# Decayed queries and keys of the retention staged for their stores in three tiles of their own

## The chip, the cores and the metric

The kernel runs on one core of a Trainium2 chip. The metric is the device time of one execution in microseconds (us): 1528.29 us before the change, the median of three runs (1525.65 to 1530.34 us).

## The reference, cut to what matters

One encoder layer over 1024 tokens of width 1024, all in float32: a mixer (dilated window attention in 8 heads beside a two-directional retention in 4 heads), a cross attention to 256 memory tokens, and a mixture of 32 experts. The change touches the first stage of the mixer, which makes the operands of the retention:

```
proj = h @ w_in                        # columns: aq, ak, av, rq, rk, rv, rg
qr = split_heads(rq)                   # 4 heads of 64
kr = split_heads(rk) * 64 ** -0.5
k_dec = exp(lg * (C - 1 - i))          # the key's decay to its chunk's end
chunk_kv = einsum(kr, k_dec, vr)
q_dec = exp(lg * (i + 1))              # the query's decay from its chunk's start
y_cross = einsum(qr, q_dec, prev)
...
```

Both decays exist forward and backward (`lg` per head and direction). The kernel makes `qr * q_dec` and `kr * k_dec` once, in the projection stage, and keeps them in DRAM until the retention heads load them.

## The kernel before, in words

Every matmul of float32 data is done in three passes over values split into a high part (rounded to the matmul's format by a copy on ScalarE, ACT) and a low part (value minus high part, a subtraction on VectorE, DVE, or on GpSimd, POOL): high times high, low times high, high times low. The helper `split` (lines 110 to 113) writes both parts; `mm3` (119 to 122) issues the three matmuls. So ACT's L112 and the subtraction's L113 stand for all splits, told apart by their tiles, and TensorE's (PE's) L120 to L122 stand for all such matmuls.

The first stage (lines 318 to 660) makes 48 units in a loop, 8 for each of the six 512-column blocks of `w_in`: queries (`unit_qk`, c = 0), keys (c = 1), values (`unit_v`, c = 2), retention queries and keys (`unit_rqk`, c = 3), retention values (`unit_rv`, c = 4) and gates (`unit_rg`, c = 5). A unit is 24 matmuls on PE into one bank of PSUM (tag "mm", five banks, used in turn), a "chain" that empties the bank, and for some a "tail" with PE transposes, traced one unit later. The weights of the next block are split by `W.split` (L116 on ACT, L117 on DVE) into the four slots that the present block's last unit sets free, pair by pair.

A unit of `unit_rqk` with j = 0 to 3 is a query unit, with j = 4 to 7 a key unit. Query unit: the bank is split into a tile `spr`, stored to `rT_s` by two DMAs; then, for each direction, DVE multiplies the bank by the decay table into `qd` (L451, a "po" tile of three), `qd` is split into a tile `spqd` (ACT, POOL) and stored to `qd_s` by four DMAs. After the second `qd` the bank is empty. Key unit: `spr` likewise, a plain copy `kf` (L447, ACT, a "po" tile too) which empties the bank, and in the tail four PE transposes of `kf` (`tkd`, L465), eight multiplications into two tiles `kd` (L471), each split into a tile `kt` (ACT, POOL) and stored to `kd_s` by one DMA (L475).

All of `spr`, `spqd`, `kt`, the value units' `vt` (six DMAs each) and the retention values' `rvt` (four each) are tiles of one tag, "sp", in the pool `st`: two buffers of 4 KB per partition, given out in turn. A tile can be written when all the DMAs that read the tile two before it have landed. All stores and loads are issued by SyncE's queue (SP) in one order.

The pool `sl` ("p1late", line 632) holds what belongs to this part of the stage, `kd` and the decay tables among it; it is closed at s_ = 33, and the next pool there ("head0", line 651) takes its place in SBUF, with the first attention head's keys, values and queries.

This stage has no order written out by hand (only its first units have). A planner at build time puts each engine's instructions in order: of what its own model takes to be ready, what stands first in the program. On the chip each engine then runs its queue strictly in that order. So the order in which PE meets the matmuls of a unit and the transposes `tkd` is the planner's.

Of the kernel before, what the change touches and what calls it, by code (L numbers as in the profile page):

```python
# [11 lines left out]
F32R = mybir.dt.float32r  # L12
# [8 lines left out]
P = 128  # L21
# [18 lines left out]
GN_EPS = 1e-5  # L40
NEG = -1e30
PADJ = 16
KW = S + 2 * PADJ


@with_exitstack
def kernel(
# [270 lines left out]
    with ExitStack() as c1:  # L318
# [47 lines left out]
        def store2(dst, src_h, src_l):  # L366
            nc.sync.dma_start(dst[0], src_h.bitcast(F32))
            nc.sync.dma_start(dst[1], src_l.bitcast(F32))

        def parts(tag, name):  # L370
            t = st.tile([P, 4, 2, P], F32R, tag=tag, name=name).rearrange("p a i c -> p (a i c)")
            return [t[:, 512 * i:512 * i + 512] for i in range(2)]

        xts = {}
# [37 lines left out]
        def side_by_side(name):  # L412

            return st.tile([P, 4, 2, P], F32R, tag="sp", name=name)
# [20 lines left out]
        def unit_rqk(c, j):  # L435
            f, half = divmod(j, 2)
            isk, rp = divmod(f, 2)
            hs = slice(512 * half, 512 * half + 512)
            ps = bank("mm", 5, f"prqk{f}{half}")
            kf = st.tile([P, 512], F32, tag="po", bufs=3, name=f"kf{f}{half}") if isk else None  # L440

            def chain():
                h, l = parts("sp", f"spr{f}{half}_")
                split(h, l, ps)
                store2([t[f * P:f * P + P, hs] for t in rT_s], h, l)
                if isk:
                    act.activation(kf, ps, AF.Copy)  # L447
                    return
                for d in range(2):
                    qd = st.tile([P, 512], F32, tag="po", bufs=3, name=f"qd{f}{half}{d}")  # L450
                    dve.tensor_tensor(qd.rearrange("p (c i) -> p c i", c=2), ps.rearrange("p (c i) -> p c i", c=2),  # L451
                                      Gq[rp][:, d][:, None, :].to_broadcast([P, 2, 256]), OP.mult)
                    h, l = parts("sp", f"spqd{f}{half}{d}_")
                    split(h, l, qd, pool)
                    for j in range(2):
                        hh = 2 * rp + j
                        rows = slice(64 * j, 64 * j + 64)
                        store2([t[P * hh + 64 * d:P * hh + 64 * d + 64, hs] for t in qd_s], h[rows], l[rows])

            def tail():  # L460
                if not isk:
                    return
                pt = bank("tr", 3, f"tkd{f}{half}")
                for i in range(4):
                    pe.transpose(pt[:, i * P:i * P + P], kf[:, i * P:i * P + P], ident)  # L465
                ptv = pt.rearrange("p (c a h d) -> p a c h d", c=2, a=2, h=2)
                for j in range(2):
                    kd = sl.tile([P, 4, 2, 64], F32, tag="kd", name=f"kd{f}{half}{j}")
                    for a in range(2):
                        for d in range(2):  # L470
                            dve.tensor_scalar(kd[:, a::2, d], ptv[:, a, :, j], Gk[rp][:, a, d, j:j + 1], None,  # L471
                                              op0=OP.mult)
                    kt = side_by_side(f"kt{f}{half}{j}")
                    split(kt[:, :, 0], kt[:, :, 1], kd.rearrange("p t d e -> p t (d e)"), pool)
                    nc.sync.dma_start(kd_s[2 * rp + j, :, 4 * half:4 * half + 4],  # L475
                                      kt.rearrange("p t i c -> p t (i c)").bitcast(F32))
            return lambda: projT(ps, W.w[c], f, half), chain, tail
# [1897 lines left out]
```

## Time and profile before

| what | value |
| --- | --- |
| median of three runs | 1528.29 us (1525.65 to 1530.34) |
| the profiled execution | 1529.57 us, span 1527.6 us |
| PE busy | 1470.6 us, 96% of the span |
| VectorE, ScalarE, GpSimd busy | 75%, 58%, 15% |
| granted PE clock, mean | 0.988 |
| first stage (projections) | 0 to about 300 us |
| retention queries and keys on PE (c = 3) | 159 to 204 us |
| experts | about 950 us to the end |

Times in all rows are microseconds from the start of the span. The profiled execution's own time is its span and 2.0 us around it.

### The profile page before, as it was taken

The numbers are of one execution on the slowest core, as the hardware profiler recorded it, in microseconds if no ns is written. First come the engines' busy times: TensorE is split into PE (matmuls) and PEld (weight loads), VectorE is DVE, ScalarE is ACT, GpSimd is POOL, SyncE is SP. The second block draws the span as 40 slices with busy tenths as digits, with TensorE's granted clock in tenths as the row PEclk, the third lists the DMA queues.
The fourth block names the chain that finished last, engine by engine and source line by source line (L and its number), as shares of the span: only waits on it lengthen the run. The fifth ranks groups of instructions, "written<-read, shape, count | busy, mean of one in ns | idle before, by whom it ended". The sixth has DMA issues, their size and how long they took to land. (4 is left out here: it accounts for less than half of the span.)

```text
span 1527.6 us, 22387 instructions
## 1 busy us (share of the span) xinstructions
PE 1470.6 (96%) x7722; PEld 1171.7 (77%) x7722; DVE 1144.2 (75%) x2557; ACT 887.7 (58%) x1493; POOL 234.7 (15%) x204
## 2 busy tenths in 40 slices
PE   8999999999989999999999998999999999999995
PEld 7788878798978877888878886777777777776663
DVE  8865355287766675978675678899898899888894
ACT  6431233298862243733352325888888888877783
POOL 0000134234310000000000002222222222221111
PEclk9999999999999999999999998999999999999998
DMA  8446775779578884621235728999999999999992
GB/s 303 112 124 193 207 232 161 207 215 253 174 216 276 321 293 134 239 100 42 60 137 201 287 96 300 337 353 362 368 377 364 357 364 370 364 358 358 364 381 84
DMA packets 129109, 383.64 MB, mean 251 GB/s; under 512 B 16288, under 2 KB 49312, under 8 KB 110560
## 3 DMA queue, kind: packets, MB, share of 16 engines
q1 hardware_dynamic: 120624, 360.27, 67.9%
q0 software_dynamic: 8368, 21.91, 5.7%
q8 instruction: 62, 1.02, 0.3%
q14 instruction: 55, 0.45, 0.1%
HBM read 318.81 MB, written 71.70 MB: 256 GB/s over the span
## 5 line engine op out<-in xcount | busy, mean ns | idle before, releaser
L120 PE MATMUL p<-eh,x 128*96 128x512 f32 x384 | 154.0, 401 | 0.0
L122 PE MATMUL p<-el,x 128*96 128x512 f32 x384 | 152.3, 396 | 0.0
L121 PE MATMUL p<-eh,x 128*96 128x512 f32 x384 | 151.8, 395 | 0.0
L1684 POOL DMA_INDIRECT xg<-h_s,idx x32 | 77.4, 2420 | 277.3 <-PE xt L1694 276.5
L113 DVE TENSOR_TENSOR el<-ews,eh 128x1024 fp32r<-128x1024 f32 x86 | 100.9, 1219 | 15.7 <-ACT eh L112 15.7
L112 ACT ACTIVATE eh<-ews 128x1024 fp32r<-128x1024 f32 x86 | 87.4, 1054 | 21.8 <-DMA ews<-in_w_down_dram 10.6
L113 DVE TENSOR_TENSOR el<-ex,eh 128x1024 fp32r<-128x1024 f32 x74 | 86.8, 1217 | 3.9 <-PE xt L1694 1.8
L122 PEld LDWEIGHTS p<-el,x 128*96 128x96 f32 x384 | 62.5, 163 | 27.1 <-issue 0.5
L121 PEld LDWEIGHTS p<-eh,x 128*96 128x96 f32 x384 | 62.7, 163 | 25.7 <-DVE x L113 0.4
L120 PEld LDWEIGHTS p<-eh,x 128*96 128x96 f32 x384 | 62.4, 162 | 24.8 <-ACT x L112 0.2
L112 ACT ACTIVATE eh<-ex 128x1024 fp32r<-128x1024 f32 x74 | 75.5, 1054 | 9.6 <-PE p L121 4.7
L1767 POOL DMA_INDIRECT out_dram<-yo,idx x32 | 51.3, 1604 | 174.0 <-ACT yo L1766 169.4
L113 DVE TENSOR_TENSOR el<-wraws,eh 128x1024 fp32r<-128x1024 f32 x60 | 70.2, 1218 | 3.0 <-ACT eh L112 2.1
L112 ACT ACTIVATE eh<-wraws 128x1024 fp32r<-128x1024 f32 x60 | 60.4, 1054 | 5.5 <-DMA wraws<-in_w_up_dram 2.6
L113 DVE TENSOR_TENSOR ehl<-ex,ehl 128x1024 fp32r<-128x1024 f32 x50 | 58.7, 1215 | 0.0
L1766 ACT ACTIVATE yo<-py,lists 96x512 f32<-96x512 f32 x64 | 42.9, 684 | 25.8 <-PE py L122 25.5
L112 ACT ACTIVATE ehl<-ex 128x1024 fp32r<-128x1024 f32 x50 | 51.9, 1058 | 6.2 <-PE py L122 5.5
L120 PE MATMUL po<-woh,mx 128*128 128x512 f32 x128 | 51.8, 405 | 3.5 <-ACT mx L112 1.8
L113 DVE TENSOR_TENSOR ehl<-ews,ehl 128x1024 fp32r<-128x1024 f32 x44 | 51.9, 1218 | 2.4 <-ACT ehl L112 2.4
L120 PE MATMUL y<-VW,pT 128*128 128x512 f32 x128 | 53.0, 414 | 0.0
L112 ACT ACTIVATE ehl<-ews 128x1024 fp32r<-128x1024 f32 x44 | 45.8, 1057 | 11.5 <-PE py L122 5.5
L120 PE MATMUL py<-ehl,hm 128*96 128x512 f32 x128 | 52.2, 408 | 0.0
(844 smaller groups left out, 4464.7 us busy)
## 6 DMA issues: line engine op xcount, KB each, us to landing
ews<-in_w_down_dram SPq DMA_DIRECT2D x30, 1024.0 KB, 14.9
wraws<-in_w_up_dram SPq DMA_DIRECT2D x23, 1024.0 KB, 11.5
ex<-in_w_up_dram SPq DMA_DIRECT2D x22, 1024.0 KB, 13.0
ews<-in_w_gate_dram SPq DMA_DIRECT2D x20, 1024.0 KB, 11.8
ex<-in_w_gate_dram SPq DMA_DIRECT2D x19, 1024.0 KB, 14.0
ex<-in_w_down_dram SPq DMA_DIRECT2D x19, 1024.0 KB, 11.6
ews<-in_w_up_dram SPq DMA_DIRECT2D x15, 1024.0 KB, 8.0
ew4s<-in_w_gate_dram SPq DMA_DIRECT2D x14, 1024.0 KB, 13.1
```

The lines of the kernel that those rows point to most:

```text
L112: act.activation(hi, src, AF.Copy)
L113: (lo_engine or dve).tensor_tensor(lo, src, hi.bitcast(F32), OP.subtract)
L120: pe.matmul(ps, ah, bh, start=first, stop=False, **kw)
L121: pe.matmul(ps, al, bh, start=False, stop=False, **kw)
L122: pe.matmul(ps, ah, bl, start=False, stop=last, **kw)
L1684: pool.indirect_dma_start(out=self.xg[0:self.ns], out_offset=None, in_=h3_s, in_offset=bass.IndirectOffsetOnAxis(ap=self.ix, axis=0), boun ...
L1766: act.activation(yo[0:ns, 512 * c:512 * c + 512], self.py[c][0:ns], AF.Identity, scale=self.gate)
L1767: pool.indirect_dma_start(out=out, out_offset=bass.IndirectOffsetOnAxis(ap=self.ix, axis=0), in_=yo[0:ns], in_offset=None, bounds_check=S ...
```

## The change

A new tag "spd" with three buffers (SPD = 3) of 4 KB per partition in the pool `sl`. The tiles `spqd` and `kt` come from it. The tiles `spr`, `vt` and `rvt`, and those of the attention's queries and keys, stay with the two buffers of "sp". No instruction and no DMA is added or taken away.

```diff
+SPD = 3
...
+        def staged(name):
+
+            return sl.tile([P, 4, 2, P], F32R, tag="spd", bufs=SPD, name=name)
+
         def parts(tag, name):
-            t = st.tile([P, 4, 2, P], F32R, tag=tag, name=name).rearrange("p a i c -> p (a i c)")
+            t = staged(name) if tag == "spd" else st.tile([P, 4, 2, P], F32R, tag=tag, name=name)
+            t = t.rearrange("p a i c -> p (a i c)")
             return [t[:, 512 * i:512 * i + 512] for i in range(2)]
...
-                    h, l = parts("sp", f"spqd{f}{half}{d}_")
+                    h, l = parts("spd", f"spqd{f}{half}{d}_")
                     split(h, l, qd, pool)
...
-                    kt = side_by_side(f"kt{f}{half}{j}")
+                    kt = staged(f"kt{f}{half}{j}")
                     split(kt[:, :, 0], kt[:, :, 1], kd.rearrange("p t d e -> p t (d e)"), pool)
```

## Rows read from the trace of the kernel before

**Rows 1.** The page's first part: busy time, share of the span and instructions of each engine.

```profile
PE 1470.6 (96%) x7722; PEld 1171.7 (77%) x7722; DVE 1144.2 (75%) x2557; ACT 887.7 (58%) x1493; POOL 234.7 (15%) x204
```

**Rows 2.** Stretches of 25 us in the first stage: length, busy time (and instructions) of each engine, granted PE clock, DMA share, GB/s.

```profile
175.00:200.00 25.00, 25.00 (x109) 20.15 (x108) 4.19 (x7) 5.12 (x9) 7.54 (x6) 1.00 0.80 249
200.00:225.00 25.00, 21.23 (x90) 16.78 (x89) 17.17 (x34) 11.38 (x19) 6.24 (x9) 0.93 0.77 223
225.00:250.00 25.00, 25.00 (x116) 20.69 (x115) 12.25 (x31) 6.78 (x11) 11.71 (x13) 1.00 0.65 219
```

**Rows 3.** What PE waited for from 0 to 330 us: the instruction that waited, what released it, us in total, times, longest.

```profile
PE tkd L465 <- ACT kf L447: 2.4, 1, 2.4
...
PE prv L120 <- DVE qd L451: 1.4, 1, 1.4
```

**Rows 4.** The stretch of 2.5 us that follows the wait of `tkd`, columns as in rows 2.

```profile
215.00:217.50 2.50, 2.50 (x8) 1.92 (x7) 1.93 (x7) 1.11 (x2) 0.33 (x1) 0.50 0.88 292
```

**Rows 5.** PE's timeline from the last retention query and key matmuls (`prqk`) over the first retention value units (`prv`): start, duration, instruction, and the idle time before it with its releaser.

```profile
203.40 0.40 PE L121 MATMUL prqk<-hTh,wil 128*128 128x512 f32 x1
203.63 0.40 PE L122 MATMUL prqk<-hTl,wih 128*128 128x512 f32 x1
205.38 0.47 PE L120 MATMUL prv<-wih,hTh 128*128 128x512 f32 x1 [1.35 <-DVE qd L451]
205.69 0.39 PE L121 MATMUL prv<-wih,hTl 128*128 128x512 f32 x1
...
210.68 0.39 PE L122 MATMUL prv<-wil,hTh 128*128 128x512 f32 x1
213.48 0.65 PE L465 MATMUL tkd<-ident,kf 128*128 128x128 f32 x4 [2.41 <-ACT kf L447]
213.89 0.48 PE L120 MATMUL prv<-wih,hTh 128*128 128x512 f32 x1
...
214.43 0.40 PE L122 MATMUL prv<-wil,hTh 128*128 128x512 f32 x1
...
218.54 0.60 PE L465 MATMUL tkd<-ident,kf 128*128 128x128 f32 x4
```

**Rows 6.** ACT's timeline, the tiles of tag "sp" and the copies `kf`.

```profile
177.17 0.63 ACT L112 ACTIVATE spqd__1861<-qd 128x512 fp32r<-128x512 f32 x1 [3.67 <-DMA vA_s<-vt]
...
185.53 0.60 ACT L112 ACTIVATE spr__1902<-prqk 128x512 fp32r<-128x512 f32 x1 [6.58 <-DMA qd_s<-spqd__1861]
...
194.37 0.60 ACT L112 ACTIVATE spr__1950<-prqk 128x512 fp32r<-128x512 f32 x1 [4.41 <-DMA qd_s<-spqd__1909]
...
211.43 0.60 ACT L112 ACTIVATE spr__2047<-prqk 128x512 fp32r<-128x512 f32 x1 [4.52 <-DMA qd_s<-spqd__2005]
212.83 0.60 ACT L447 ACTIVATE kf<-prqk 128x512 f32<-128x512 f32 x1 [0.80 <-DVE spr__2047 L113]
...
215.93 0.60 ACT L447 ACTIVATE kf<-prqk 128x512 f32<-128x512 f32 x1 [1.33 <-DVE spr__2079 L113]
```

**Rows 7.** DVE's timeline: the decayed queries of units 0, 1, 2 and 3, and the last four low parts of the weights of block 4.

```profile
174.14 1.28 DVE L451 TENSOR_TENSOR qd<-prqk,Gq 128x512 f32<-128x512 f32 x2
...
186.77 1.28 DVE L451 TENSOR_TENSOR qd<-prqk,Gq 128x512 f32<-128x512 f32 x2
...
195.61 1.28 DVE L451 TENSOR_TENSOR qd<-prqk,Gq 128x512 f32<-128x512 f32 x2
200.63 2.81 DVE L117 SCALAR_TENSOR_TENSOR wil<-wi,mixw_t,wih 128x512 fp32r<-128x512 f32 x4 [3.74 <-ACT wih L116]
...
203.96 1.28 DVE L451 TENSOR_TENSOR qd<-prqk,Gq 128x512 f32<-128x512 f32 x2
205.16 4.81 DVE L117 SCALAR_TENSOR_TENSOR wil<-wi,mixw_t,wih 128x512 fp32r<-128x512 f32 x4
```

**Rows 8.** SP's queue: four of the eight stores of unit 2's decayed queries, issued back to back.

```profile
200.21 0.54 SPq L367 DMA_DIRECT2D qd_s<-spqd__1966  x1
...
202.09 0.59 SPq L368 DMA_DIRECT2D qd_s<-spqd__1966  x1
```

**Rows 9.** DMA issues by tile from 150 to 260 us: number, KB each, median us from issue to landing.

```profile
kd_s<-kt SPq DMA_DIRECT2D x8, 512.0 KB, 3.2
...
qd_s<-spqd__1861 SPq DMA_DIRECT2D x4, 128.0 KB, 5.5
...
qd_s<-spqd__2005 SPq DMA_DIRECT2D x4, 128.0 KB, 2.2
```

**Rows 10.** POOL's timeline: low parts of decayed queries without and with DVE's weight splits beside them, and head 0's key tile at the place of `p1late`.

```profile
198.81 1.28 POOL L113 TENSOR_TENSOR spqd__1966<-qd,spqd__1966 128x512 fp32r<-128x512 f32 x1 [0.45 <-ACT spqd__1966 L112]
...
206.15 1.57 POOL L113 TENSOR_TENSOR spqd__2005<-qd,spqd__2005 128x512 fp32r<-128x512 f32 x1 [2.48 <-DMA rT_s<-spr__1998]
207.68 1.74 POOL L113 TENSOR_TENSOR spqd__2014<-qd,spqd__2014 128x512 fp32r<-128x512 f32 x1
...
244.57 0.11 POOL L252 MEMSET K<- 128x16 f32 x1
```

**Rows 11.** Later stretches, columns as in rows 2.

```profile
650.00:750.00 100.00, 100.00 (x555) 86.91 (x554) 75.99 (x292) 37.00 (x94) 0.00 (x0) 1.00 0.15 57
1000.00:1350.00 350.00, 350.00 (x1666) 249.23 (x1665) 314.14 (x317) 296.71 (x356) 88.50 (x40) 1.00 1.01 366
```

**Rows 12.** What SP's queue waited for from 800 us to the end.

```profile
SPq L1648 <- DVE el L113: 345.4, 122, 7.2
```

## The prediction

> **What bounds the kernel now.** I read the page's busy times first: PE is busy 96% of the span, the next engine 75% [rows 1]. So an edit off PE pays only where PE stands still or runs at the lower clock. The table of stretches shows where that is near the change: PE is busy 25.00 of 25 us before 200 us and after 225 us, and 21.23 between, with a mean granted clock of 0.93 there [rows 2]. The list of PE's waits names two: the first `prv` unit waits 1.4 us for `qd` (it needs the bank that query unit 3 still holds), the first `tkd` 2.4 us for `kf`, the copy out of key unit 4 [rows 3]. After the second, the granted clock is 0.50 for a stretch of 2.5 us, PE's lower level of 1.2 GHz [rows 4].
>
> PE's timeline prices it [rows 5]. A `prv` matmul follows the one before it after (210.68 − 205.69) / 22 = 0.227 us. Undisturbed, `prv` unit 0 would start at 203.63 + 0.23 = 203.86, `tkd` 24 × 0.227 = 5.44 later at 209.30, and after its 0.41 and the thirteen `prv` matmuls that lie between, 2.95, the second `tkd` at 212.66. It starts at 218.54: 5.88 us are lost. Of these 205.38 − 203.86 = 1.52 are the first wait, 213.48 − 210.91 = 2.57 the second, 0.17 the slow first matmul after each, and 218.54 − 214.43 less 11 × 0.227 = 1.61 the lower clock. The clock fell after the idle of 2.57 and not after that of 1.52.
>
> Both waits come from one queue of tiles. ACT's timeline shows it: each split waits for the stores of the tile two before it, 6.58 us before unit 1's `spr`, 4.41 before unit 2's, 4.52 before unit 4's [rows 6]. So the `qd` pairs of units 0 to 3 start at 174.14, 186.77, 195.61 and 203.96, steps of 12.6, 8.8 and 8.4 us [rows 7], while PE makes a unit in 24 × 0.23 = 5.5 us [rows 5]. The chain falls behind until all five banks are full.
>
> **The change part by part.** No instruction goes or comes; every tile of `spqd` and `kt` changes its buffer.
>
> The query chain. A split of `qd` now waits for the third `spqd` before it, and `spr` only for the `spr` two before it. Per tile of three: ACT 0.63 [rows 6], POOL 1.28 [rows 10], four issues on SP at (202.09 − 200.21) / 3 = 0.63 each [rows 8], and 2.2 to 5.5 from issue to landing [rows 9]: 0.63 + 1.28 + 2.52 + 5.5 = at most 9.9 us for three tiles, 6.6 for a unit's two. SP's own pace is about the same: a unit's ten stores take at most 10 × 0.63 = 6.3 us. That is more than PE's 5.5 and less than the 8.4 to 12.6 of before. From 174.14 the fourth pair of `qd` then starts at 174.14 + 3 × 6.6 = 193.9 and ends at 195.2. From the other side, nothing gained, it ends at 205.2 as now. I take 195.2, as the rows are of these very tiles. Then bank 3 is free 8.7 us before PE wants it at 203.86, and the first wait, 1.52 + 0.08, is gone.
>
> The key chain. `kf` of unit 4 follows a unit later, by about 195.2 + 6.6 = 201.8; it ends at 213.43 now [rows 6]. PE's place for the first `tkd`, if it stays behind `prv` unit 0, is 209.30: 7.5 us to spare. So the second wait goes (2.57 + 0.09), and the lower clock with it (1.61). If the place moves, see the rivals.
>
> What is late next: the low parts of the weights that `prv` reads. DVE's last four end at 209.97, 1.20 us each against 0.70 for the four before [rows 7]; the slow ones lie beside two POOL subtractions that take 1.57 and 1.74 instead of 1.28 [rows 10]. If PE starts 1.5 us earlier, the matmul that reads the last low part is due at 203.86 + 23 × 0.227 = 209.1: up to 0.9 us of a new wait, or nothing if the `qd` work that stands beside them has moved away. I take 0.4.
>
> The Trainium skill, "SBUF — State Buffer", section "Who interferes with whom", has the general rule: a DVE instruction with two inputs in SBUF contends with a GpSimd instruction that reads SBUF, and the one that comes second is blocked. By it the cost grows with the number of POOL subtractions that fall on the splits, and the change brings eight more of them, those of `kt`, nearer to that place. The rows above agree in direction; by the rule the sum would be that of rival B.
>
> What is moved, and queued behind. SP gets the same 32 stores of `qd` and eight of `kd` in the same mutual order, only earlier; the loads of head 0 stand behind later stores and come no later. A longer life: `p1late` lies where head 0's keys come to lie, and its tiles are now read by DMAs, not only by POOL. The `K` memset at 244.57 [rows 10] then waits for a landing, 3.2 us [rows 9], behind the last `kt`; POOL's `rvt` subtractions and SP's loads queue behind it. But the last `kt` comes earlier by what unit 4's `kf` gains, 213.4 − 201.8 = 11.6 us, so this costs nothing; were that cover gone it would cost up to 3.2, the length of that landing.
>
> Does the gain reach the end? Later PE is busy 100.00 of 100 and 350.00 of 350 us [rows 11], and the loads of expert weights wait for DVE to free their tiles [rows 12], so they move with the work and nothing stands at a fixed time. The shift passes through.
>
> Sum: 5.88 − 0.4 = 5.5 us off the profiled 1529.57 us, 1524.1. That execution lies 1.3 above the median of the runs; off the median it is 1522.8 us.
>
> **The rivals.**
> A. The transposes wait again. The planner puts `tkd` where it takes `kf` to be ready. In the order before it was ahead of the chip: undisturbed, the first two `tkd` would have stood at 209.30 and 212.66 and their `kf` ended at 213.43 and 216.53, 4.1 and 3.9 us later [rows 5, 6]. With an earlier `kf` it may place `tkd` earlier too and keep its lead. A lead of 4.1 costs 4.1 + 1.8 for clock and first matmuls = 5.9: nothing is gained, 1528.3. A lead of 2 costs 2 to 3.8: 1524.4 to 1526.2. For it: two cases in this very place. Against: three buffers leave less for a lead to gather, and PE's waits in this stage besides are few.
> B. POOL's `kt` subtractions fall on the weight splits. If all eight low parts take 1.20 instead of 0.70, the last is 2.0 later than now, and PE waits about 2.9 at the end of `prv` unit 0: 5.9 − 2.9 = 3.0 gained, 1525.3; with a drop of the clock behind it, 1.6, only 1.4: 1526.9. For it the slow rows; against, that a unit has only two `kt`.
> C. Slower: the planner puts `tkd` directly behind the next unit's matmuls, its place in the program. Unit 5 ends on PE at 203.86 − 2 × 5.5 = 192.8, `kf` of unit 4 comes at the 201.8 of above: PE stands 9.0 us in front of it, and with 1.8 behind loses 10.8 against 5.9 now: 4.9 slower, 1533.2. It decides from a lead of 4.1 us, and reaches 0.3% at 8.7. If the chain does not get faster than now, `kf` is there at 213.4 and the price is up to 16 us. For it: PE takes its queue in order and nothing else of PE's could pass. Against: five free banks keep PE's earlier matmuls ready, so a planner that sees `kf` late fills the place with them.
> D. The change does not do what it says: the chain stays at its 8.4 us a unit although it has its buffers, because SP's issues pace it. The row gives 6.3 for them; if it did, the waits stay, 1528.3.
>
> **How the numbers follow.** About 0.3% (4.6 us) is what a measurement of this kernel can tell from no change. Forecast, 4.6 to 6 us gained: 0.48. A and B, both less than 4.6 gained: 0.22 and 0.09, D 0.03. C: 0.18, a third of it, 0.06, with leads between 4.1 and 8.7 us that stay within 0.3%. So faster 0.48, same 0.22 + 0.09 + 0.03 + 0.06 = 0.40, less 0.04 for the few of A that gain 4.6 and more, which go to faster: 0.52, 0.36 and 0.12. The range: below, 5.88 gained and about 2 more if head 0's start tightens with earlier stores, 1520; above, C reaches 1533 and more, and with less than 2 in 10 left out the range stops at 1530.5. The likeliest case alone spans 1522 to 1524.
>
> **What would show it.** Right: in the stretch of 200 to 225 us PE busy 25.0 and clock 1.00; no wait of `prv` for `qd` and none of `tkd` for `kf`; ACT's waits of 4 to 7 us before `spr` gone; `qd` pairs 5.5 to 6.5 us apart; the last projection matmul 5 to 6 us earlier, and the end by as much. Wrong: a `tkd` row with an idle over 2 us before it and a stretch of clock 0.50 behind it (A or C, told apart by the place of `tkd` among the units); slow `wil` rows with PE waiting for DVE (B); `qd` pairs still 8 us apart (D); or a shift of 5 us at 300 us that is no longer there at 1000.

## The result: 0.7% slower, and the profile after

The changed kernel takes 1542.43 us, the median of five runs (1537.25 to 1544.37); the kernel before, run beside it, 1530.16 (1525.65 to 1532.4). The ratio is 1.0073 with a 95% interval of 1.0052 to 1.0094: 8 to 14 us slower. The forecast was 1522.8, its range ended at 1530.5. The profiled execution after the change took 1544.37 us with a span of 1542.5, 14.9 longer than the span of before; it was the slowest of the five. Of all executions behind this text one, of the run e1 below, took 1637.09 us at a granted clock of 0.841; the ratios leave it out, and without it the median of e1 is 1533.22 us instead of 1533.45. Where the 14.9 us come from is read off PE's marks in the two profiles:

| us from the start of the span | before | after | later by |
| --- | --- | --- | --- |
| first `prqk` matmul (c = 3 begins) | 159.1 | 160.5 | 1.4 |
| first `prv` matmul (c = 4) | 205.4 | 205.3 | -0.1 |
| last `prg` matmul (projections end) | 299.7 | 301.8 | 2.1 |
| first `oA` matmul (head 0 of the attention) | 304.5 | 315.1 | 10.6 |
| last `sA` matmul | 414.2 | 428.1 | 13.9 |
| last matmul of the experts | 1499.1 | 1514.1 | 15.0 |

So c = 3 first wins 1.5 us (of 1.4 late to 0.1 early), loses 2.2 again up to the end of the projections, and the large loss of 8.5 lies in the 13 us in which the attention starts. The 1.4 us at the first mark are not the change's: in e1, e6 and e9 below, which hold the same three tiles, c = 3 begins at 159.1 or 159.2. Another 3.3 us come between the first `oA` and the last `sA`; some 1.1 of them are the lower clock up to 320 us (5 us at a mean of 0.78), the rest was not traced. Lines of the changed kernel stand one further than before from 43 to 367 and six further from 380 on (L112 to L114 are the helper `split`, L117 and L118 the weights' parts, L471 `tkd`, L513 `porg`).

The stretches of 25 us, columns as in [rows 2]: length, busy time of PE, PEld, DVE, ACT and POOL (with instructions), granted clock, DMA share, GB/s.

```profile
200.00:225.00 25.00, 22.83 (x104) 18.25 (x102) 15.42 (x30) 11.26 (x19) 7.87 (x6) 1.00 0.57 179
225.00:250.00 25.00, 22.93 (x99) 18.65 (x98) 12.05 (x31) 5.86 (x10) 9.08 (x11) 0.93 0.79 284
300.00:325.00 25.00, 16.39 (x108) 15.40 (x107) 11.61 (x42) 12.66 (x39) 6.73 (x15) 0.80 0.83 244
```

The hole of [rows 2] between 200 and 225 us is now two smaller ones, of 2.2 us before and 2.1 us after 225 us. And from 300 to 325 PE stands still for 8.6 us. What PE waited for from 0 to 330 us, columns as in [rows 3]:

```profile
PE sA L824 <- DVE nn L827: 8.6, 1, 8.6
PE tkd L471 <- ACT kf L453: 4.1, 2, 2.1
```

`prv` no longer waits for `qd`. `tkd` waits twice instead of once, and longer in sum (4.1 against 2.4). New in size is one wait of `sA`, the scores of head 0, for `nn`, the row statistics that DVE takes of the scores. The same wait before, and DVE's wait for the stores of the gates before it:

```profile
PE sA L818 <- DVE nn L821: 1.1, 1, 1.1
...
DVE porg L507 <- DMA rg_s<-porg: 4.0, 2, 3.8
```

**The retention stage.** DVE's timeline, the lines that answer to [rows 7]:

```profile
175.27 1.28 DVE L457 TENSOR_TENSOR qd<-prqk,Gq 128x512 f32<-128x512 f32 x2
...
179.37 1.28 DVE L457 TENSOR_TENSOR qd<-prqk,Gq 128x512 f32<-128x512 f32 x2
...
187.20 1.28 DVE L457 TENSOR_TENSOR qd<-prqk,Gq 128x512 f32<-128x512 f32 x2
202.09 3.56 DVE L118 SCALAR_TENSOR_TENSOR wil<-wi,mixw_t,wih 128x512 fp32r<-128x512 f32 x5 [13.61 <-ACT wih L117]
206.03 3.69 DVE L118 SCALAR_TENSOR_TENSOR wil<-wi,mixw_t,wih 128x512 fp32r<-128x512 f32 x3 [0.39 <-ACT wih L117]
```

The decayed queries of all four query units are out of their banks by 188.5 us (unit 2's two come singly, from 181.16 on), not 205.2 as before. The buffers do what they are there for. But what follows on ACT does not come:

```profile
185.97 0.60 ACT L113 ACTIVATE spr__1998<-prqk 128x512 fp32r<-128x512 f32 x1 [1.06 <-DMA rT_s<-spr__1902]
201.33 3.53 ACT L117 ACTIVATE wih<-wi,mixw_t 128x512 fp32r<-128x512 f32 x5 [14.77 <-PE prqk L123]
204.76 0.62 ACT L113 ACTIVATE spqd__1966<-qd 128x512 fp32r<-128x512 f32 x1
...
207.13 0.62 ACT L113 ACTIVATE spqd__2005<-qd 128x512 fp32r<-128x512 f32 x1
...
210.42 0.60 ACT L453 ACTIVATE kf<-prqk 128x512 f32<-128x512 f32 x1 [2.18 <-DVE spr__2047 L114]
210.91 0.62 ACT L113 ACTIVATE spqd__2014<-qd 128x512 fp32r<-128x512 f32 x1
...
218.61 0.60 ACT L453 ACTIVATE kf<-prqk 128x512 f32<-128x512 f32 x1 [3.49 <-DVE spr__2079 L114]
...
226.79 0.60 ACT L453 ACTIVATE kf<-prqk 128x512 f32<-128x512 f32 x1 [4.44 <-DVE vmean L492]
```

ACT stands still for 14.77 us in front of `wih`, the high parts of block 4's weights, which wait for PE's last key unit to free their tiles. Behind the first five of them in the queue stand the sixth to eighth `spqd`, whose `qd` are long there, and all four `kf`. In the kernel before six `spqd` stood ahead of `wih`, in this one five. `kf` of units 4 to 6 come at 210.42, 218.61 and 226.79 us, and the transposes wait for the second and third, 2.07 us each. The last link of these two waits is on DVE:

```profile
217.22 0.69 DVE L491 TENSOR_REDUCE vmean<-prv 128x4 f32<-128x512 f32 x1 [2.22 <-PE prv L123]
217.83 0.68 DVE L114 TENSOR_TENSOR spr__2079<-prqk,spr__2079 128x512 fp32r<-128x512 f32 x1
```

`vmean`, a mean that DVE takes of the value unit just ended, waits for PE, and the low part of unit 5's `spr`, whose high part ACT had begun at 214.54, stands behind it. `kf` follows that low part and PE follows `kf`: two steps of DVE and one of ACT, while PE stands still. The same 2.07 us stand twice in e1, e6, e9 and e13 too. The clock behind the two waits, in stretches of 2.5 us (length, busy PE, granted clock, DMA share, GB/s):

```profile
220.00:222.50 2.50, 2.50 (x13) 1.00 0.79 307
225.00:227.50 2.50, 0.43 (x3) 1.00 0.00 0
227.50:230.00 2.50, 2.50 (x10) 0.69 0.81 315
230.00:232.50 2.50, 2.50 (x11) 0.63 0.77 301
```

It stays at full speed behind the first and is partly at its lower level (0.50, 1.2 GHz) behind the second: 5 us at a mean of 0.66 cost 1.7. With the 4.1 of the waits this is 5.8 us, about what the stage lost before (5.88): from the last `prqk` to the last `prg` it takes 301.8 - 205.1 = 96.7 us, 96.1 before.

**The start of the attention.** SP's queue lies otherwise too. Before, SP issued the two weight loads of block 5 and the four key loads of head 1 in gaps of the retention stage, up to 224.43 us:

```profile
187.28 0.45 SPq L181 DMA_DIRECT2D wi<-in_w_in_dram  x1
...
204.45 0.47 SPq L271 DMA_DIRECT2D K<-kT_s  x1
...
224.43 0.45 SPq L271 DMA_DIRECT2D K<-kT_s  x1
```

After the change the weight loads stand at 235 us and head 1's key loads between the fourth and the fifth gate store:

```profile
235.26 1.38 SPq L182 DMA_DIRECT2D wi<-in_w_in_dram  x2
...
287.86 0.90 SPq L514 DMA_DIRECT2D rg_s<-porg  x2
288.86 1.16 SPq L269 DMA_DIRECT2D QB<-qT_s  x2
290.07 2.51 SPq L272 DMA_DIRECT2D K<-kT_s  x4
292.63 0.58 SPq L275 DMA_DIRECT2D vA<-vA_s  x1
293.31 0.85 SPq L514 DMA_DIRECT2D rg_s<-porg  x2
294.33 1.58 SPq L269 DMA_DIRECT2D QB<-qT_s  x2
296.61 5.66 SPq L272 DMA_DIRECT2D K<-kT_s  x4
302.52 2.08 SPq L514 DMA_DIRECT2D rg_s<-porg  x3
...
311.05 0.32 SPq L514 DMA_DIRECT2D rg_s<-porg  x1
```

The gates `porg` (DVE's product with `th`, the tanh that ACT takes of a gate unit) are written into "po" tiles, three in turn, so the sixth, seventh and eighth wait until the third, fourth and fifth have landed. DVE's timeline (the 8 `porg`, then the scores):

```profile
291.47 0.69 DVE L513 SCALAR_TENSOR_TENSOR porg<-th,prg 128x512 f32<-128x512 f32 x1 [0.19 <-DMA rg_s<-porg]
...
302.55 1.41 DVE L513 SCALAR_TENSOR_TENSOR porg<-th,prg 128x512 f32<-128x512 f32 x2 [9.05 <-DMA rg_s<-porg]
310.33 0.69 DVE L513 SCALAR_TENSOR_TENSOR porg<-th,prg 128x512 f32<-128x512 f32 x1 [6.37 <-DMA rg_s<-porg]
310.94 0.42 DVE L827 CUSTOM_DVE_ANT_0 sA<-sA,bA 128x256 f32<-128x256 f32 x1
```

The fifth gate is written at 292.2 us; its store is issued at 302.52, behind head 1's loads, and has landed when the eighth `porg` starts at 310.33. How much of this is the place in the queue and how much the load on the DMA engines (a share of 1.02 to 1.05 from 295 to 320 us) was not separated. DVE takes its queue in order, so `nn` stands behind the eighth `porg`, and PE behind `nn`.

### The profile page after: what moved, and what is told of

Same layout as the page of the kernel before. It is cut to its first block, busy times and chain, and to the rows that moved or that the text cites. A ratio compares the mean times of both kernels' runs of the same rounds, so it can differ in the third digit from the quotient of the medians.

```text
span 1542.5 us, 22369 instructions
## 1 busy us (share of the span) xinstructions
PE 1478.6 (96%) x7722; PEld 1179.5 (76%) x7722; DVE 1143.9 (74%) x2557; ACT 886.4 (57%) x1493; POOL 232.1 (15%) x204
## 3 DMA queue, kind: packets, MB, share of 16 engines
q8 instruction: 62, 1.02, 0.3%
## 5 line engine op out<-in xcount | busy, mean ns | idle before, releaser
L114 DVE TENSOR_TENSOR el<-ews,eh 128x1024 fp32r<-128x1024 f32 x86 | 101.0, 1220 | 15.9 <-ACT eh L113 15.8
L114 DVE TENSOR_TENSOR el<-ex,eh 128x1024 fp32r<-128x1024 f32 x74 | 86.9, 1218 | 6.3 <-ACT eh L113 6.3
L114 DVE TENSOR_TENSOR el<-wraws,eh 128x1024 fp32r<-128x1024 f32 x60 | 70.3, 1220 | 2.7 <-ACT eh L113 2.7
L114 DVE TENSOR_TENSOR ehl<-ex,ehl 128x1024 fp32r<-128x1024 f32 x50 | 58.7, 1215 | 0.0
L117 ACT ACTIVATE wih<-wi,mixw_t 128x512 fp32r<-128x512 f32 x48 | 31.6, 716 | 45.9 <-PE prv L122 15.0
L118 DVE SCALAR_TENSOR_TENSOR wil<-wi,mixw_t,wih 128x512 fp32r<-128x512 f32 x48 | 35.6, 782 | 27.5 <-ACT wih L117 27.5
L114 DVE TENSOR_TENSOR ehl<-ews,ehl 128x1024 fp32r<-128x1024 f32 x44 | 51.9, 1218 | 3.0 <-ACT ehl L113 3.0
## 6 DMA issues: line engine op xcount, KB each, us to landing
ex<-in_w_gate_dram SPq DMA_DIRECT2D x19, 1024.0 KB, 14.9
```

What stands on the lines that cost most here:

```text
L114: (lo_engine or dve).tensor_tensor(lo, src, hi.bitcast(F32), OP.subtract)
L117: act.activation(hi, src, AF.Identity, scale=scale)
L118: dve.scalar_tensor_tensor(lo, src, scale, hi.bitcast(F32), op0=OP.mult, op1=OP.subtract)
```

## The experiments

All times are medians in us; "before" is the kernel before, run in the same set on the same chip. The changed kernel itself (1542.43) ran beside a before of 1530.16; the sets differ by up to 1.3 us there, and the five runs of the changed kernel by 7. So a gain of 2 to 4 us against it, as of e3, e13 and e14, cannot be told by the time alone; there the waits in the profile decide. The diffs are cut (...); they stand against the changed kernel, or, where said, against the kernel before.

| run | us | before | ratio, 95% interval |
| --- | --- | --- | --- |
| e1 gate tiles | 1533.45 | 1531.41 | 1.0018 (1.0005 to 1.0031) |
| e2 gate tiles, kernel before | 1531.93 | 1531.41 | 1.0007 (0.9991 to 1.0022) |
| e3 loads early | 1540.03 | 1531.41 | 1.0059 (1.0042 to 1.0076) |
| e4 ACT's order | 1535.64 | 1531.41 | 1.0022 (1.0005 to 1.0039) |
| e5 late loads, kernel before | 1533.59 | 1530.07 | 1.0020 (1.0005 to 1.0036) |
| e6 head 1's loads last | 1542.65 | 1530.07 | 1.0082 (1.0059 to 1.0106) |
| e7 ACT's order and gate tiles | 1531.82 | 1530.07 | 1.0015 (0.9998 to 1.0033) |
| e8 queries alone | 1534.97 | 1530.07 | 1.0033 (1.0019 to 1.0047) |
| e9 third value split | 1542.57 | 1529.67 | 1.0079 (1.0061 to 1.0097) |
| e10 all orders and gate tiles | 1526.21 | 1529.67 | 0.9973 (0.9961 to 0.9986) |
| e11 the same, kernel before | 1531.83 | 1529.67 | 1.0010 (0.9996 to 1.0024) |
| e12 keys alone | 1528.25 | 1529.67 | 0.9991 (0.9978 to 1.0004) |
| e13 gate stage's order | 1539.62 | 1529.46 | 1.0064 (1.0052 to 1.0077) |
| e14 gate stage's order, loads early | 1538.46 | 1529.46 | 1.0049 (1.0031 to 1.0066) |

### Does the wait for gate tiles cost the large part? (e1, e2)

```diff
-                o = st.tile([P, 512], F32, tag="po", bufs=3, name=f"porg{f}_{half}")
+                if j in (5, 6):
+                    o = st.tile([P, 1024], F32, tag="sp", name=f"porg{f}_{half}")[:, 0:512]
+                else:
+                    o = st.tile([P, 512], F32, tag="po", bufs=3, name=f"porg{f}_{half}")
```

> The changed kernel, with two of the eight gate tiles (porg) taken from the tag sp, idle by then, so that no porg waits for the landing of an rg_s store. Theory 1 (the loss is made at head 0's start: head 1's key loads now stand among the gate stores, the stores land late, porg waits for its tile, and DVE's queue holds head 0's first reduction behind it): PE's wait of 8.6 us for nn falls under 2 us, head 0's first block (first sA to first oA) takes about 5 us instead of 13, and the time falls by 7 to 10 us against the changed kernel, to 1532 to 1536. Theory 2 (the loss is made in the retention stage, where ACT's queue now holds a decayed query behind the weight splits): the wait for nn does not matter, the time stays at 1540 to 1544. Rival 3 (the loss is spread over later stages by transfers that collide): the wait goes, but less than 3 us of the time.

The same edit on the kernel before, e2:

> The kernel before with the same two gate tiles from sp, as the control of the run above. Its wait for nn is 1.1 us only. Theory 1: at most 1 to 2 us faster than before, 1527 to 1531. Theory 2 and rival 3: the same, 1528 to 1532. A gain of 5 us or more would say that the tiles, and not the place of head 1's loads, are the point.

With two more gate tiles the changed kernel wins 9.0 us of its 12; the kernel before wins nothing. PE's waits in e1:

```profile
PE tkd L471 <- ACT kf L453: 4.1, 2, 2.1
PE sA L827 <- POOL K L254: 1.7, 1, 1.7
...
PE sA L827 <- DVE nn L830: 0.4, 1, 0.4
```

The wait for `nn` is gone, the retention stage's is what it was. So the chain "landing of a gate store, DVE's queue, `nn`, PE" carries the large loss, and the stage in which the change was made is not where it costs.

### Which loads make the landings late? (e3, e5, e6)

e3 moves the loads back to an early place:

```diff
-            if j == (2 if c == 0 else 0) and c < 5:
+            if j == (2 if c == 0 else 0) and c < 4:
                 W.load(c + 1)
+            if s_ == 25:
+                W.load(5)
+            if s_ == 32:
+                K1 = [t[:, 0:KW] for t in first_slots("K1_")]
+                key_pads(K1)
+                k_loads(1, K1)
...
```

> The changed kernel, with the loads of weight block 5 traced a block earlier (at unit 1 of the retention queries) and head 1's key loads at the start of the retention values, so that neither stands among the gate stores of 288 to 303 us. ACT's order in the retention stage stays that of the changed kernel. Theory 1: rg_s stores land in about 4 us as before, the wait for nn falls under 2 us, the time falls by 7 to 10 us to 1532 to 1536, like the run with gate tiles. Theory 2: no change, 1540 to 1544. Rival 3: 2 to 4 us faster.

A miss: 1540.03. The wait of `sA` for `nn` halves (4.1), but the moved loads shift the planner's orders once more, and `prv` now waits 4.2 us for a decayed query on ACT. One edit changed two things, so it could not tell them apart. e5 does the reverse on the kernel before, with one edge and nothing else:

```diff
+            lq = nc.sync.dma_start(QB[64 * i:64 * i + 64, :].bitcast(F32), qT_s[i][rows, :])
+        with tc.issue_after(lq.ins) if hd == 1 else ExitStack():
+            for i in range(2):
+                for j in range(2):
+                    nc.sync.dma_start(K[i][64 * j:64 * j + 64, PADJ:PADJ + S].bitcast(F32), kT_s[i][rows, :])
```

> The kernel before with one edge more: the four K loads of head 1 may be issued only behind head 1's two QB loads, so that SP issues them between the sixth and the seventh gate store, where the changed kernel has them; the weight loads of block 5, head 0's loads and all else stay. Theory 1 (the place of head 1's key loads among the gate stores holds up porg, and with it nn and PE): DVE's wait of porg for the landing of rg_s grows from 4.0 us to 10 to 20, PE's wait of sA for nn from 1.1 to 5 to 9, and the kernel gets 4 to 9 us slower than before: 1535 to 1540 us against 1531.4. Rival (the landings are late because the whole first stage stands later or otherwise, and four loads more between the stores do not matter): both waits stay within 1 us of before, 1531.4 within 2.

Four loads in another place of a queue (between the fourth and the fifth gate store, which is where the changed kernel has them) make the kernel before 3.1 us slower (0.8 to 5.5), and `porg` waits 18.2 us for landings, nearly as after the change (19.5). DVE's timeline of e5 and PE's wait:

```profile
296.07 0.69 DVE L508 SCALAR_TENSOR_TENSOR porg<-th,prg 128x512 f32<-128x512 f32 x1 [7.91 <-DMA rg_s<-porg]
...
303.93 0.69 DVE L508 SCALAR_TENSOR_TENSOR porg<-th,prg 128x512 f32<-128x512 f32 x1 [6.21 <-DMA rg_s<-porg]
```

```profile
PE sA L819 <- DVE nn L822: 3.8, 1, 3.8
```

The mechanism is shown; of the size it gives a part, a wait of 3.8 us where there was 1.1, against 8.6 after the change, so something else made the gates later still. e6 takes head 1's loads out of the way at the other end, behind the last gate store:

```diff
...
-            if s_ == 43:
-                head1 = head_loads(1, None)
+            if s_ == 47:
+                with tc.issue_after(rgst[-1]):
+                    head1 = head_loads(1, None)
```

> The changed kernel, with all six loads of head 1 (two QB, four K) issued behind the last gate store; head 0's loads stay between the stores. Theory 1: the wait of porg for the landing of rg_s falls from 19.5 us to 10 or less, PE's wait of sA for nn from 8.6 to 1 to 3, and the kernel gains 5 to 8 of the 12 us: 1534 to 1538 us against 1542.4, unless head 1 then waits for its own loads (PE waiting for QB or K in the stretch of 330 to 420 us would say so). Rival (head 0's loads or the stores themselves are the jam, as the run with early K loads may mean, in which porg still waited 14.8): porg waits 15 us or more and the time stays at 1540 to 1542.

Here the second of the two waits of `porg` is gone (the sixth to eighth go together at 301.08, after 10.24 us) and `sA` waits only 2.1 us for `nn`. The time stays at 1542.65, since head 1 then waits for the loads that were pushed back:

```profile
PE sA L827 <- DMA K<-kT_s: 7.3, 2, 5.6
...
PE sA L827 <- DVE nn L830: 2.1, 1, 2.1
```

### The rest: ACT's order in the gate stage (e9, e13, e14)

Next to the loads, the third, fourth and fifth value split `rvt` stood one place further back in ACT's queue than before. e9 puts back the third alone:

```diff
...
-                for i in range(4):
-                    W.split(c + 1, i)
+                with tc.issue_after(last_rv) if c == 4 else ExitStack():
+                    for i in range(4):
+                        W.split(c + 1, i)
             chain()
+            if s_ == 34:
+                last_rv = spl[-1]
```

> The changed kernel with one edge more: ACT's weight splits of block 5 stay behind the third value split, rvt, which the planner had put behind the first two of them (before the change it stood ahead of all eight). All other queues but DVE's two low parts beside it stay as they are. Theory 1b (the gate chain is late by this rvt too: POOL's third rvt at 255 instead of 248 us, the first porg at 279.4 instead of 271.7, and the late chain then meets the loads of heads 0 and 1): the first porg comes at 273 to 275 us, PE's wait of sA for nn falls from 8.6 to 3.5 to 6, and the kernel gains 3 to 5 us: 1537 to 1539. Rival (the place of head 1's key loads alone makes the last porg late): nothing moves, 1541 to 1543.

A miss, 1542.57: the third `rvt` comes 7 us earlier on POOL (248.19 against 255.06), but the fourth (264.54) stands behind the first `th`, as in the changed kernel, and the first `porg` stays at 279.76 (279.43 after the change). A late chain moves only if all its links do. e13 puts back the fourth and the fifth too; its edges on the sixth to eighth hold in the changed kernel as it is:

```diff
...
-            chain()
+            with tc.issue_after(rv[s_ - 39]) if 40 <= s_ < 45 else ExitStack():
+                chain()
+            if 34 <= s_ < 40:
+                rv.append(spl[-1])
```

> The changed kernel with ACT's order of the gate stage put back to that of the kernel before: the third value split ahead of block 5's weight splits, and each of the five later ones ahead of the gate th that it stood behind by one place. SP's queue and all else stay as changed. Theory 1b, put rightly this time (the run with the third split alone only moved the queue to the fourth, which stood behind the first th): POOL's fourth rvt comes at 257 to 260 us instead of 264, the first porg at 272 to 275 instead of 279.4; the late loads of head 1 remain, so porg still waits for landings, but PE's wait of sA for nn falls from 8.6 to 3.5 to 6 as in the two other runs with an early chain and late loads (3.8 and 5.7): 1536.5 to 1540. Rival (ACT's order there has no part in it): 1541 to 1544, sA waits 8 or more.

1539.62, and the first `porg` at 272.84, 6.6 us earlier. PE's wait:

```profile
PE sA L830 <- DVE nn L833: 5.3, 1, 5.3
```

e14 is e13 with the early loads of e3:

> The same order of ACT's gate stage, and the loads of block 5 and of head 1's keys early as in the run that moved these loads alone (1540.0 us, first stage about 5 us later than after the change, sA waiting 4.1 for nn). Theory (late chain and late loads are the whole of the second loss): sA waits 1.5 us at most, and the kernel gains 3 to 4 us on that run: 1536 to 1537.5; what it then lacks to the kernel before, 5 to 7 us, is the first stage alone (prg's last matmul at 305 to 307 us against 299.7). Rival (something else slows the landings): sA waits 3 us or more, 1539 to 1541.

```profile
PE sA L840 <- DVE nn L843: 1.4, 1, 1.4
```

The wait is as short as forecast; the time, 1538.46, is 1 us above it and between what theory and rival gave. The wait decides for the theory: of the 8.6 us, 3.3 are ACT's order (8.6 to 5.3) and 3.9 the place of the loads (5.3 to 1.4), which leaves the 1.1 of before and 0.3. The rest that e14 lacks is in the first stage: its last `prg` matmul begins at 306.1 us, 5.3 later than in e13, and the first `porg` is later by the same 5.3. The other runs bear this out. Either the first `porg` starts 27.9 or 28.0 us ahead of the last `prg`, as before the change, or 22.3 or 22.4; and head 1's key loads lie either ahead of the gate stores or among them:

| wait of `sA` for `nn`, us | loads early | loads late |
| --- | --- | --- |
| gates early | 1.1 (before), 1.1 (e8), 1.4 (e14) | 3.8 (e5), 5.7 (e4), 5.3 (e13) |
| gates late | 4.1 (e3) | 8.6 (after), 8.9 (e9) |

### What the tiles give when the orders are right (e4, e7, e10, e11)

e4 keeps ACT's splits of block 4 behind the last decayed query:

```diff
...
-                for i in range(4):
-                    W.split(c + 1, i)
+                with tc.issue_after(last_qd) if c == 3 else ExitStack():
+                    for i in range(4):
+                        W.split(c + 1, i)
             chain()
+            if s_ == 27:
+                last_qd = spl[-1]
```

> The changed kernel, with ACT's high parts of weight block 4 kept behind the last decayed query of unit 3 (an order on ACT's queue only); SP's order stays that of the changed kernel. Theory 2: ACT's wait of 14.8 us in front of the weight splits no longer holds a decayed query, the kf are there before 200 us, the waits of tkd and the half clock behind them go, PE's last projection matmul comes 5 to 7 us earlier, and the time falls to 1524 to 1530. Theory 1: the retention stage gains those 5 to 7 us at most, the wait for nn of 8 us stays, and the time is 1533 to 1538. If the wait for nn eats what the stage gains (its stores and loads move with SP, not with PE): 1539 to 1543.

`tkd` no longer waits for `kf`, and the time falls by 6.8 us to 1535.64. A new wait comes in its place: `prv` 2.9 us for `wil`. `sA` still waits 5.7 for `nn`. With the one edge on ACT the planner also put DVE's low part of unit 5's `spr` ahead of `vmean` and the third to fifth value split back to their places, so e4 does not tell ACT's part in the waits from DVE's. e7 adds the gate tiles of e1 to it:

> The changed kernel with both cures together: ACT's weight splits of block 4 kept behind the last decayed query, and two of the eight gate tiles in a queue of tiles of their own. If the two losses are independent, the gains add: 9.0 us from the gate tiles, and from ACT's order 6.8 less the 2.9 by which its run already had a shorter wait of sA for nn, 3.9; 1542.4 - 12.9 = 1529.5, 1.9 us under the kernel before at 1531.4. If my first reckoning of the first stage was right after all (5.5 us to be had there), it is 1525 to 1527. If the two act on the same microseconds, it stays at 1533 to 1536. PE's wait of sA for nn at most 1 us, none of tkd for kf, one of prv for wil of about 2.9.

1531.82, between the sum of the two gains and the case that they overlap. The 2.9 us stay, and DVE's timeline of e7 says why:

```profile
204.68 2.16 DVE L479 TENSOR_SCALAR kd<-tkd,Gk 128x128 f32<-128x128 f32 x8 [11.71 <-PE tkd L473]
206.75 4.98 DVE L120 SCALAR_TENSOR_TENSOR wil<-wi,mixw_t,wih 128x512 fp32r<-128x512 f32 x6
```

The same trap on the next engine: eight `kd`, which wait for PE's transposes, stand ahead of six low parts, the first of which have had their data since 200.7 us. e10 puts `kd` behind them and uses the fourth and fifth gate instead of the sixth and seventh:

```diff
...
+            if s_ == 31:
+                for k in kds:
+                    tc.add_manual_dep(k, wil[-1].name, mybir.DependencyInfo(
+                        mybir.DependencyClass.NoSync, mybir.DependencyReason.DATA), reason="kd")
...
```

> The changed kernel with ACT's splits of block 4 behind the last decayed query, two gate tiles (the fourth and fifth now, not the sixth and seventh) in tiles of their own, and a new order on DVE: the kd scalings, which wait for PE's transposes, stay behind the eight low parts of block 4's weights. Theory (the 2.9 us wait of prv for wil in the run with both cures comes from DVE's queue, where eight kd stood ahead of six low parts and DVE stood still for 11.7 us; the wait of 1.7 us for POOL's K memset came from the late gate tiles): both waits go, and 1.6 of half clock behind the first: 6.2 us off that run, about 1525.5, which is the gain of 4 to 6 us over the kernel before that the prediction had for the change. Rival (the low parts are late by themselves, since block 4's high parts wait for PE's last query unit): prv waits 2 us or more for wih or wil still, and the time stays at 1529 to 1532.

1526.21, the one version faster than both kernels: 0.27% (0.14 to 0.39) under the kernel before. Its stretches, columns as above:

```profile
200.00:225.00 25.00, 25.00 (x119) 20.64 (x118) 18.16 (x46) 13.22 (x22) 8.32 (x7) 1.00 0.55 196
225.00:250.00 25.00, 25.00 (x113) 20.68 (x111) 11.25 (x23) 5.97 (x10) 6.10 (x13) 1.00 0.68 230
```

No hole and no lower clock. From the last `prqk` to the last `prg` it takes 294.8 - 204.6 = 90.2 us, 5.9 less than before. Some 1.7 of these go again in front of `sA`, which waits for POOL to write the borders of a key tile; there my expectation was wrong, the wait does not come from which gates have the two tiles. It stands in e1, e2, e7 and e10, which have two gates in "sp", and in no run without them; e11 has the tiles and not the wait. What orders it so was not tried. e11 is e10 without the three tiles (the kernel before with the same orders and gate tiles):

> The kernel before, without the three tiles, with the same three orders and gate tiles as the run beside it. It tells whether the three tiles are worth anything once the orders are right. Theory (the tiles are needed: with two shared ones the query chain takes 8 us a unit, so block 4's splits, now behind the last decayed query at about 206 us, come late and prv waits for them): prv waits 4 us or more for wih or wil, and the time is 1532 to 1536 us. Rival (the orders do it alone): as fast as the run beside it, within 2 us.

```profile
PE prv L122 <- ACT wih L118: 3.6, 1, 3.6
```

1531.83, no gain: with two shared buffers the last decayed query is split on ACT at 206.83 us, and block 4's weights, now behind it, come late. With the same orders the three tiles are worth 5.6 us (1531.83 to 1526.21). So the tiles pay, but only with the orders; these orders alone are worth nothing.

### One half of the change at a time (e8, e12)

e8 takes the queries' tiles alone, e12 the keys' alone:

```diff
-                    kt = staged(f"kt{f}{half}{j}")
+                    kt = side_by_side(f"kt{f}{half}{j}")
```

> The part of the change that concerns the queries alone: the eight spqd tiles in the three buffers, the eight kt tiles back with the spr tiles. In the order of its queues ACT still has the last decayed queries behind the weight splits of block 4, but SP's loads of block 5 and of head 1's keys lie in gaps early on, as before the change. By my two theories it therefore has the first loss and not the second: PE waits for kf in front of tkd about 4 us as after the change, prv starts without a wait, sA waits for nn at most 2 us, and the time is 1530 to 1535 us. Rival (the tiles of the change themselves, or the stores that they let come earlier, slow the gate stores' landings): sA waits 5 us or more and the time is 1538 to 1543.

```diff
-                    h, l = parts("spd", f"spqd{f}{half}{d}_")
+                    h, l = parts("sp", f"spqd{f}{half}{d}_")
```

> The part of the change that concerns the keys alone: the eight kt tiles in the three buffers, the eight spqd tiles back with the spr tiles. ACT has six decayed queries ahead of block 4's weight splits again, SP's loads of block 5 lie in their gaps, two of head 1's key loads lie among the gate stores. By the theories: the first loss does not come (the query chain and its waits as before the change, prv for qd 1.4 and tkd for kf about 2.4), the second comes by half at most, sA waits for nn 1 to 4 us; 1529 to 1533. Rival (any tile taken from the spr queue reorders the stage badly): 1536 or more.

PE's waits of e8:

```profile
PE tkd L471 <- ACT kf L453: 6.4, 2, 4.3
...
PE sA L824 <- DVE nn L827: 1.1, 1, 1.1
```

The first loss without the second, 1534.97, as expected: in e8 the loads lie in gaps early on. The first loss is larger here than in the changed kernel, 101.6 us from the last `prqk` to the last `prg`; but the profiled execution, 1539.11, was the slowest of its twelve. DVE's part is plain in it: the high part of unit 5's `spr` is done at 211.64 us, and its low part starts at 216.70, behind `vmean`. e12 has neither (`prv` 1.4 for `qd`, `tkd` 2.4 for `kf`, `sA` 1.1 for `nn`, all as before) and 1528.25, no change that can be told. So the first loss comes with the queries' tiles alone; the second shows only with both halves of the change.

## Why the prediction was wrong

**What bounds the kernel: right.** The 5.88 us read from PE's timeline [rows 5] are there to be had: e10 gets 5.9 of them.

**The query chain: right, and faster than I took it.** The fourth pair of `qd` was to end at 195.2; it ends at 188.5. Bank 3 is free, and `prv` starts 0.23 us behind the last `prqk`, without a wait.

**The key chain: the first step that failed.** I let `kf` of unit 4 follow a unit after the queries, at 201.8 us, as if ACT took a split when its data and its buffer are there. ACT takes it when it is at the head of its queue, and there stood five `wih` that wait for PE's last key unit. `kf` came at 210.42, only 2.4 earlier than before. The first `tkd` then hardly waited, but the next two did, 4.1 us together, behind the `vmean` on DVE, which I had not looked at; 1.7 of lower clock came behind them. So the 2.57 and the 1.61 that my sum took as gone were lost again in another place. In e10, where the queues are right, `kf` of unit 4 comes at 194.14 and no `tkd` waits. I had read ACT's timeline only for the tiles of "sp" [rows 6]; the `wih` between them, and what would stand on either side of them, decided. That is rival A's outcome (the transposes wait again, nothing gained in the stage) by other queues: what came late was ACT's and DVE's work, and PE's place for `tkd` was not moved ahead.

**"No instruction goes or comes", "the same mutual order": the second step that failed, and the dear one.** Of SP I wrote that the loads of head 0 "come no later", and costed it at nothing. I counted the stores that the change moves, not the loads that lived in the gaps between them. In its new order the planner (why was not shown) put head 0's key loads at 290.07 us instead of 283.57, block 5's weight loads at 235 us instead of 175 and 187, and head 1's key loads at 296.61 instead of 204.45 to 224.43, into the gate stores. And that this place is tight was to be seen before: three gate tiles, and a wait of DVE for their landing of 3.8 us that no PE wait showed. PE waited 8.6 us, 7.5 more than before, and had the lower clock behind it (granted 0.80 from 300 to 325 us). By e13 and e14, 3.9 of these 7.5 are the place of the loads and 3.3 ACT's order, the third to fifth value split that the planner put back: an order too that I had taken to stay.

**"The shift passes through": only in part for a gain, right for a loss.** I looked for a fixed time after 650 us [rows 11, 12]; the place where a shift is taken up lies at 300 us, where DVE's queue stands between the projections and the attention: of the 4.9 us by which the last `prg` of e10 is earlier than before, 2.9 are left at the first `oA` (301.6 against 304.5). What is late there (13.9 us at the last `sA`) is late at the end (15.0).

**The late low parts: not what I priced.** After the change `prv` does not wait for `wil`, so the 0.4 of my sum measured nothing. The slow rows are there: the last three low parts take 3.69 us, 1.23 each on average, beside two POOL subtractions of 1.35, the five before 0.71 each. The Trainium skill, "SBUF — State Buffer", section "Who interferes with whom", says that a DVE instruction with two inputs in SBUF contends with a GpSimd instruction that reads SBUF; the direction agrees here as in [rows 7, 10], and the seven low parts of e10 with no POOL work beside them take 0.71 each. That price is small. The 2.9 us of e4 and e7 came from DVE's order, not from the port. Rival B was not it.

**Rivals C and D.** C named the right sign and the wrong place: the transposes were not put too far ahead, and the stage as a whole lost 0.6 us against before (96.7 to 96.1). D did not happen.

**The chances.** Slower had 0.12, all of it with rival C. Every rival was about the stage of the change; none asked what a new order does at the next narrow place. A change of which tile waits for which is also a change of every queue that a planner fills, and that belonged in the range.

## What to carry to other kernels

More buffers for one chain change the input of whatever orders the queues: compare the order of every engine's queue before and after, the DMA issues too, and look for an instruction that waits long in front of others that are ready. If the new order puts work behind a wait, say the order by hand; here the buffers with two such edges and two more gate tiles gave 3.5 us where the buffers alone cost 12. And look for tiles that are given back by a landing, on an engine whose next work PE needs: there a DMA issued some places later in SP's queue became a wait of PE.

## What the runs showed of the hardware

The granted clock answered the same idle time differently: behind two waits of 2.07 us each it stayed at 1.00 once and fell to a mean of 0.66 over 5 us once in the profile after. The same two waits of 2.07 us stand in e1, e6 and e9, and there the means of the stretches from 217.5 to 222.5 and from 227.5 to 232.5 us are 0.66 and 0.66 in e1 and e9, 0.66 and 1.00 in e6. So these two waits with the clock behind them lost 5.8 us in one execution and 7.5 in another.

A store waited longer in SP's queue than for its landing: between 294.33 and 302.27 us SP was taken up by six loads of head 1, and the four key loads took 5.66 us where those of head 0 took 2.51; SP's own waits there are 2.1 us for the landing of `vA` and 2.4 for that of earlier key loads. The fifth gate's store spent 10.4 us in SP's queue (292.2 to 302.52) and 7.8 from issue to landing. The Trainium skill, "DMA: Bandwidth & Descriptors", section "Issuing engines are not separate DMA queues", holds that issuing from several engines saves only the sequencer's time, usually small beside the transfer itself. Here the time in the queue was the longer of the two, but it was not the issuing of this one store: it was the six loads ahead of it and their waits for landings. Whether issuing the gate stores from another engine would have saved it was not tried.
